# Short-sequence attention on one core: four rows of a head per partition, float32 loads rounded on GpSimd, eight heads per exp

## The chip, the cores and the metric

The kernel runs on one core of a Trainium2 chip. A core has five engines with queues of their own: TensorE (PE, with its weight loads listed apart as PEld), VectorE (DVE), ScalarE (ACT), GpSimd (POOL) and SyncE (SP, which here only issues DMAs). Data lie in SBUF and PSUM, both of 128 partitions; PSUM has 8 banks of 2 KB per partition, and matmuls write only there. The metric is the time of one execution in microseconds (us), the median of several.

## The reference

32 batches of 12 heads, sequence length 128, head size 64, all float32:

```python
scale = 1.0 / np.sqrt(q.shape[-1])
scores = scale * np.matmul(q, k.transpose(0, 1, 3, 2))
scores_max = np.max(scores, axis=-1, keepdims=True)
attn = np.exp(scores - scores_max)
attn = attn / (np.sum(attn, axis=-1, keepdims=True) + 1e-8)
return np.matmul(attn, v).astype(np.float32)
```

The inputs are small (a normal draw times 0.1), so both kernels leave out the maximum.

## The kernel before

It loops over the 32 batches. In each, three DMAs from GpSimd's queue bring q, k and v of all 12 heads to SBUF and round them to bfloat16 on the way (`q_bf`, `k_bf`, `v_bf`, 128 partitions, one sequence row of every head per partition, so a DMA moves pieces of 64 float32 values, 256 B). `v_bf` has a 65th column of ones per head; its matmul gives the sum of the exponentials for free.

Two heads at a time are transposed on PE (`qt_ps`, `kt_ps`, one buffer each in PSUM) and copied to SBUF, q by ACT (L68) and k by DVE (L75). For groups of 4 heads the scores are formed, keys on partitions, with a contraction of 64 (L84, `sT_ps`, four PSUM banks, one buffer); one exp on ACT takes the four heads (L92, `attnT`). The output matmuls (L103) go two heads at a time into `o_ps` (two banks, one buffer), and DVE copies them out to `o_b` (L110). At the end of a batch come a reciprocal of the sums (L116), a multiply (L118) and one store from SP's queue (L119).

The order on each engine is not that of the text. The framework's scheduler lays all instructions out in advance, by the order of the text as priority and by what its model of the engines says is ready, and puts in all semaphores; PE therefore mixes transposes of the next batch with scores and outputs of this one. At run time each engine follows that fixed order.

Of the kernel before, what the change touches and what calls it, by code (L numbers as in the profile page):

```python
# [1 line left out]

# [5 lines left out]


@with_exitstack
def kernel(
    ctx: ExitStack,
    tc: tile.TileContext,
    q: bass.AP,
    k: bass.AP,
    v: bass.AP,
    out: bass.AP,
):
    nc = tc.nc  # L20
    f32 = mybir.dt.float32
    bf16 = mybir.dt.bfloat16

    B, H, S, D = q.shape
    assert S == 128 and D == 64
    scale = 1.0 / (D ** 0.5)
    HT = 128 // D
    NP = H // HT
    HX = 4
    HO = 2  # L30
    BANK = 512

    qr = q.rearrange("b h s d -> b s h d")
    kr = k.rearrange("b h s d -> b s h d")
    vr = v.rearrange("b h s d -> b s h d")
    orr = out.rearrange("b h s d -> b s h d")

    singles = ctx.enter_context(tc.tile_pool(name="singles", bufs=1))
    ident = singles.tile([128, 128], bf16)
    make_identity(nc, ident)  # L40

    pbf = ctx.enter_context(tc.tile_pool(name="pbf", bufs=3))
    pt = ctx.enter_context(tc.tile_pool(name="pt", bufs=3))
    pa = ctx.enter_context(tc.tile_pool(name="pa", bufs=6))
    po = ctx.enter_context(tc.tile_pool(name="po", bufs=2))
    ps_t = ctx.enter_context(tc.tile_pool(name="ps_t", bufs=1, space=bass.MemoryType.PSUM))
    ps_s = ctx.enter_context(tc.tile_pool(name="ps_s", bufs=1, space=bass.MemoryType.PSUM))
    ps_o = ctx.enter_context(tc.tile_pool(name="ps_o", bufs=1, space=bass.MemoryType.PSUM))

    for b in range(B):  # L50
        q_bf = pbf.tile([128, H, D], bf16, tag="q_bf")
        nc.gpsimd.dma_start(out=q_bf, in_=qr[b])  # L52
        k_bf = pbf.tile([128, H, D], bf16, tag="k_bf")
        nc.gpsimd.dma_start(out=k_bf, in_=kr[b])  # L54
        v_bf = pbf.tile([128, H, D + 1], bf16, tag="v_bf")
        nc.gpsimd.memset(v_bf[:, :, D:D + 1], 1.0)  # L56
        nc.gpsimd.dma_start(out=v_bf[:, :, :D], in_=vr[b])  # L57

        qt = pt.tile([128, NP, 128], bf16, tag="qt")
        kt = pt.tile([128, NP, 128], bf16, tag="kt")  # L60
        for p in range(NP):
            qt_ps = ps_t.tile([128, 128], bf16, tag="qt_ps")
            nc.tensor.transpose(  # L63
                qt_ps,
                q_bf[:, p * HT:(p + 1) * HT, :].rearrange("a b c -> a (b c)"),
                ident,
            )
            nc.scalar.copy(qt[:, p, :], qt_ps)  # L68
            kt_ps = ps_t.tile([128, 128], bf16, tag="kt_ps")
            nc.tensor.transpose(  # L70
                kt_ps,
                k_bf[:, p * HT:(p + 1) * HT, :].rearrange("a b c -> a (b c)"),
                ident,
            )
            nc.vector.tensor_copy(kt[:, p, :], kt_ps)  # L75

        o_b = po.tile([128, H, D + 1], f32, tag="o_b")

        for g in range(H // HX):
            sT_ps = ps_s.tile([128, HX, BANK], f32, tag="sT")  # L80
            for i in range(HX):
                h = g * HX + i
                p, j = divmod(h, HT)
                nc.tensor.matmul(  # L84
                    sT_ps[:, i, :128],
                    lhsT=kt[j * D:(j + 1) * D, p, :],
                    rhs=qt[j * D:(j + 1) * D, p, :],
                    start=True,
                    stop=True,
                )  # L90
            attnT = pa.tile([128, HX, 128], bf16, tag="attnT")
            nc.scalar.activation(  # L92
                out=attnT,
                in_=sT_ps[:, :, :128],
                func=mybir.ActivationFunctionType.Exp,
                bias=0.0,
                scale=scale,
            )
            for gg in range(HX // HO):
                o_ps = ps_o.tile([128, HO, BANK], f32, tag="o_ps")  # L100
                for i in range(HO):
                    h = g * HX + gg * HO + i
                    nc.tensor.matmul(  # L103
                        o_ps[:, i, :D + 1],
                        lhsT=attnT[:, gg * HO + i, :],
                        rhs=v_bf[:, h, :],
                        start=True,
                        stop=True,
                    )
                nc.vector.tensor_copy(  # L110
                    o_b[:, g * HX + gg * HO:g * HX + (gg + 1) * HO, :],
                    o_ps[:, :, :D + 1],
                )

        recip = po.tile([128, H], f32, tag="recip")
        nc.vector.reciprocal(recip, o_b[:, :, D:D + 1])  # L116
        o_sb = po.tile([128, H, D], f32, tag="o_sb")
        nc.vector.tensor_mul(o_sb, o_b[:, :, :D], recip.to_broadcast([128, H, D]))  # L118
        nc.sync.dma_start(out=orr[b], in_=o_sb)  # L119


# [1 line left out]
_INS = ['q', 'k', 'v']  # L123
_OUTS = [((32, 12, 128, 64), 'float32')]


# [23 lines left out]
```

## Time and profile before

| | |
|---|---|
| median of 3 runs | 226.65 us (226.57 to 226.68) |
| span of the profiled execution, first to last instruction | 224.4 us |
| its own time beside the span | not listed apart; the median is 2.25 us above the span |
| PE busy | 168.3 us (75%), 1152 matmuls |
| DVE, ACT, POOL busy | 120.2, 99.7, 101.5 us |
| granted TensorE clock | 1.000 |
| HBM read, written | 37.75, 12.58 MB |

A row of a group reads: line, engine, operation, output and inputs by the program's names, shapes, count, then busy time in us and the mean of one in ns, then the idle time of the engine just before these instructions and what ended it. A row of the timeline reads: start in us, length in us, engine, line, operation, names, shapes, how many were merged into the row. A row of the waits reads: who waited for whom, us in total, times, longest. For PE `64*128` is the part of the array in use, rows by columns. A matmul's length holds the time that its data take to pass the array, so lengths of matmuls overlap, and their starts tell more. A row by windows reads: stretch, its length, busy time and count for each engine, granted clock, DMA share, GB/s.

### The profile page before, as it was taken

What the parts mean: (1) busy time and instruction counts of PE and PEld (TensorE: products, weight loads), DVE (VectorE), ACT (ScalarE), POOL (GpSimd) and SP (SyncE); (2) the same over time, 40 slices, a digit from 0 to 9 for tenths busy, and PEclk for the clock granted to TensorE, in tenths of its full rate; (3) what the DMA queues carried; (4) which work ended last, traced back from release to release, by engine and by line L of the source; (5) the groups of instructions that cost most, each with busy time, mean ns of one, the idle gap of its engine ahead of it and who ended that gap; (6) DMA issues with size and microseconds to landing.
All of it is one profiled execution on the core that took longest, in us unless ns stands there. A gap on an engine that the chain in (4) does not pass through costs nothing.

```text
span 224.4 us, 3513 instructions
## 1 busy us (share of the span) xinstructions
PE 168.3 (75%) x1152; PEld 83.1 (37%) x1152; DVE 120.2 (54%) x448; ACT 99.7 (44%) x289; POOL 101.5 (45%) x134
## 2 busy tenths in 40 slices
PE   0688787788787787877787877788877778878750
PEld 0344333344333343333343333444333334333330
DVE  0264555664555564555564555565555565456652
ACT  2554545445544445444445444444444444444320
POOL 8963455534475443455443455543355534222000
DMA  7999999999999999999999999999999999999333
GB/s 50 149 156 184 148 142 140 155 148 166 151 153 161 161 159 166 148 149 141 129 151 167 146 148 134 137 154 167 149 146 144 135 150 161 142 110 134 76 69 71
DMA packets 198674, 31.69 MB, mean 141 GB/s; under 512 B 198656, under 2 KB 198656, under 8 KB 198656
## 3 DMA queue, kind: packets, MB, share of 16 engines
q0 software_dynamic: 148992, 18.88, 131.9%
q1 hardware_dynamic: 49664, 12.58, 31.0%
q8 instruction: 9, 0.15, 0.3%
q14 instruction: 9, 0.07, 0.1%
HBM read 37.75 MB, written 12.58 MB: 224 GB/s over the span
## 4 chain that ended last, share of the span: by engine, by line
PE 64%; ACT 17%; DVE 9%; issue 6%; DMA 2%; ACTq 0%; POOL 0%; POOLq 0%
PE sT_ps L84 26%; PE qt_ps L63 14%; PE o_ps L103 14%; PE kt_ps L70 11%; ACT attnT L92 9%; ACT qt L68 7%; DVE o_b L110 5%; DVE kt L75 3%; DMA q_bf<-in_q_dram 2%; DVE o_sb L118 1%; ACTq L92 0%; DVE recip L116 0%; POOL ident masks.py:197 0%; POOLq masks.py:199 0%; POOLq L134 0%
## 5 line engine op out<-in xcount | busy, mean ns | idle before, releaser
L68 ACT COPY qt<-qt_ps 128x128 bf16<-128x128 bf16 x192 | 50.4, 263 | 69.0 <-PE qt_ps L63 69.0
L75 DVE COPY kt<-kt_ps 128x128 bf16<-128x128 bf16 x192 | 42.8, 223 | 70.8 <-PE kt_ps L70 66.1
L84 PE MATMUL sT_ps<-qt,kt 64*128 64x128 bf16 x384 | 71.5, 282 | 12.2 <-ACT attnT L92 11.5
L92 ACT ACTIVATE attnT<-sT_ps 128x512 bf16<-128x512 f32 x96 | 57.3, 597 | 47.7 <-PE sT_ps L84 42.9
L63 PE MATMUL qt_ps<-ident,q_bf 128*128 128x128 bf16 x192 | 54.2, 282 | 26.8 <-ACT qt L68 21.4
L110 DVE COPY o_b<-o_ps 128x130 f32<-128x130 f32 x192 | 55.6, 289 | 29.2 <-PE o_ps L103 28.9
L103 PE MATMUL o_ps<-v_bf,attnT 128*128 128x65 bf16 x384 | 56.8, 242 | 6.1 <-DVE o_b L110 6.1
L70 PE MATMUL kt_ps<-ident,k_bf 128*128 128x128 bf16 x192 | 56.4, 294 | 5.3 <-DVE kt L75 4.5
L84 PEld LDWEIGHTS <-kt 64*128 64x128 bf16 x384 | 26.4, 101 | 61.1 <-issue 43.0
L103 PEld LDWEIGHTS <-attnT 128*128 128x128 bf16 x384 | 34.3, 120 | 34.4 <-issue 26.5
L56 POOL MEMSET v_bf<- 128x12 bf16 x32 | 5.0, 155 | 79.9 <-PE o_ps L103 79.9
L52 POOL DMA_DIRECT2D q_bf<-in_q_dram x32 | 32.6, 1020 | 10.2 <-PE qt_ps L63 8.9
L57 POOL DMA_DIRECT2D v_bf<-in_v_dram x32 | 32.6, 1018 | 9.9 <-POOL v_bf L56 9.9
L54 POOL DMA_DIRECT2D k_bf<-in_k_dram x32 | 32.8, 1025 | 1.4 <-PE kt_ps L70 1.4
L63 PEld LDWEIGHTS <-q_bf 128*128 128x128 bf16 x192 | 18.9, 113 | 31.4 <-issue 15.7
L118 DVE TENSOR_TENSOR o_sb<-o_b,recip 128x768 f32<-128x768 f32 x32 | 30.3, 948 | 0.0
L70 PEld LDWEIGHTS <-k_bf 128*128 128x128 bf16 x192 | 23.2, 121 | 8.7 <-issue 0.9
L116 DVE RECIPROCAL recip<-o_b 128x12 f32<-128x12 f32 x32 | 7.0, 219 | 0.0
L68 ACT ACT_TABLE_LOAD x1 | 1.3, 1283 | 0.7 <-PEq L134 0.7
masks.py:199 POOL TENSOR_SCALAR_AFFINE_SELECT ident<-ident 128x128 bf16<-128x128 bf16 x1 | 0.3, 305 | 0.1
masks.py:197 POOL MEMSET ident<- 128x128 bf16 x1 | 0.2, 204 | 0.3 <-POOLq L134 0.3
L134 POOL MEMSET const-float32-0.0<- 128x1 f32 x1 | 0.1, 98 | 0.2 <-issue 0.2
(3 smaller groups left out, 0.3 us busy)
## 6 DMA issues: line engine op xcount, KB each, us to landing
out_dram<-o_sb SPq DMA_DIRECT2D x32, 384.0 KB, 5.7
q_bf<-in_q_dram POOLq DMA_DIRECT2D x32, 192.0 KB, 5.9
k_bf<-in_k_dram POOLq DMA_DIRECT2D x32, 192.0 KB, 6.4
v_bf<-in_v_dram POOLq DMA_DIRECT2D x32, 192.0 KB, 5.1
```

The costliest lines, as they stand in the source:

```text
L52: nc.gpsimd.dma_start(out=q_bf, in_=qr[b])
L54: nc.gpsimd.dma_start(out=k_bf, in_=kr[b])
L57: nc.gpsimd.dma_start(out=v_bf[:, :, :D], in_=vr[b])
L63: nc.tensor.transpose(qt_ps, q_bf[:, p * HT:(p + 1) * HT, :].rearrange("a b c -> a (b c)"), ident,)
L68: nc.scalar.copy(qt[:, p, :], qt_ps)
L70: nc.tensor.transpose(kt_ps, k_bf[:, p * HT:(p + 1) * HT, :].rearrange("a b c -> a (b c)"), ident,)
L75: nc.vector.tensor_copy(kt[:, p, :], kt_ps)
L84: nc.tensor.matmul(sT_ps[:, i, :128], lhsT=kt[j * D:(j + 1) * D, p, :], rhs=qt[j * D:(j + 1) * D, p, :], start=True, stop=True,)
L92: nc.scalar.activation(out=attnT, in_=sT_ps[:, :, :128], func=mybir.ActivationFunctionType.Exp, bias=0.0, scale=scale,)
L103: nc.tensor.matmul(o_ps[:, i, :D + 1], lhsT=attnT[:, gg * HO + i, :], rhs=v_bf[:, h, :], start=True, stop=True,)
L110: nc.vector.tensor_copy(o_b[:, g * HX + gg * HO:g * HX + (gg + 1) * HO, :], o_ps[:, :, :D + 1],)
L118: nc.vector.tensor_mul(o_sb, o_b[:, :, :D], recip.to_broadcast([128, H, D]))
```

## The change

All four tensors are viewed as slabs: 4 neighbouring rows of a head in each partition (1 KB in one piece), 4 heads in 128 partitions. A load brings 4 slabs (16 heads) of q, k or v as float32, 512 KB, from SP's queue, two loads ahead. GpSimd rounds them to bfloat16, q and k in two instructions each, so that two slabs lie side by side, v in one. The unit of work is then 8 heads (2 slabs), 48 units in all.

In `front(u)` eight transposes fill one PSUM bank (`qk_ps`) and DVE copies it out in one instruction (`qkT`). The transposed columns of a head come in the order (row within the partition, partition). Keys need the same order in v, so 16 matmuls with 32 columns of the identity as weights select and place the rows of v in `v_ps`; ACT copies them to `v_e`, whose columns of ones were written once. Eight score matmuls fill two banks (`s_ps`, two buffers), and one exp on ACT takes all 8 heads. In `back(u - 1)` the output matmuls of the unit before run, 32 of them, each with 32 columns of `attnT` as weights and 65 columns of `v_e`, so that the result lies as the slabs do. Reciprocal and multiply read PSUM directly, and a store of 16 heads follows every second unit.

The core of the diff, with the copies and views of the old kernel cut:

```diff
-    for b in range(B):
-        q_bf = pbf.tile([128, H, D], bf16, tag="q_bf")
-        nc.gpsimd.dma_start(out=q_bf, in_=qr[b])
...
+    def load(l):
+        sl = slice(l * LU * US, (l + 1) * LU * US)
+        got = []
+        for nm, src in (("q_f", qs), ("k_f", ks), ("v_f", vs)):
+            t = pf.tile([128, LU * US, R * D], f32, tag=nm)
+            nc.sync.dma_start(out=t, in_=src[:, sl, :])
+            got.append(t)
+        loaded[l] = got
...
+        for nm, src in (("q_b", q_f), ("k_b", k_f)):
+            t = pb.tile([128, LU * UP, R, 2, D], bf16, tag=nm)
+            for ab in range(2):
+                nc.gpsimd.tensor_copy(
+                    t[:, :, :, ab, :],
+                    src.rearrange("p (i ab) (r d) -> p i ab r d", ab=2, r=R)[:, :, ab, :, :],
+                )
+            got.append(t)
+        t = pb.tile([128, LU * US, R * D], bf16, tag="v_b")
+        nc.gpsimd.tensor_copy(t, v_f)
...
+        qk_ps = ps_t.tile([128, 2, UP, R, R, SP], bf16, tag="qk_ps")
+        for j, src in enumerate((q_b, k_b)):
+            for i in range(UP):
+                for r in range(R):
+                    nc.tensor.transpose(
+                        qk_ps[:, j, i, :, r, :],
+                        src[:, w * UP + i, r, :, :].rearrange("p a d -> p (a d)"),
+                        ident,
+                    )
+        qkT = pt.tile([128, 2, UP, R, 128], bf16, tag="qkT")
+        nc.vector.tensor_copy(qkT, qk_ps.rearrange("p j i h r s -> p j i h (r s)"))
+
+        v_ps = ps_v.tile([128, R, US, D], f32, tag="v_ps")
+        for h in range(R):
+            for r in range(R):
                 nc.tensor.matmul(
+                    v_ps[r * SP:(r + 1) * SP, h, :, :],
+                    lhsT=ident[:, h * SP:(h + 1) * SP],
+                    rhs=v_b[:, w * US:(w + 1) * US, r * D:(r + 1) * D],
                     start=True,
                     stop=True,
                 )
+        v_e = v_es[u % NVE]
+        nc.scalar.copy(v_e[:, :, :, :D], v_ps)
+
+        s_ps = ps_s.tile([128, 2, UP, R, 128], f32, tag="s_ps")
+        for i in range(UP):
+            for h in range(R):
+                for ab in range(2):
+                    pr = slice(ab * D, (ab + 1) * D)
                     nc.tensor.matmul(
+                        s_ps[:, ab, i, h, :],
+                        lhsT=qkT[pr, 1, i, h, :],
+                        rhs=qkT[pr, 0, i, h, :],
                         start=True,
                         stop=True,
                     )
+        attnT = pa.tile([128, 2, UP, R, 128], bf16, tag="attnT")
+        nc.scalar.activation(out=attnT, in_=s_ps, func=EXP, bias=0.0, scale=scale)
+        stage[u] = (v_e, attnT)
...
+        o_ps = ps_o.tile([128, 2, 512], f32, tag="o_ps")
+        for b2 in range(2):
+            for c in range(4):
+                n, r = divmod(b2 * 4 + c, R)
+                i, ab = divmod(n, 2)
+                for h in range(R):
+                    nc.tensor.matmul(
+                        o_ps[h * SP:(h + 1) * SP, b2, c * (D + 1):(c + 1) * (D + 1)],
+                        lhsT=attnT[:, ab, i, h, r * SP:(r + 1) * SP],
+                        rhs=v_e[:, h, n, :],
+                        start=True,
+                        stop=True,
+                    )
+        o4 = o_ps[:, :, :4 * (D + 1)].rearrange("p b (c e) -> p b c e", e=D + 1)
+        recip = po.tile([128, 2, 4], f32, tag="recip")
+        nc.vector.reciprocal(recip, o4[:, :, :, D])
+        nc.vector.tensor_mul(
+            o_sb[:, w].rearrange("p (b c) d -> p b c d", b=2),
+            o4[:, :, :, :D],
+            recip.unsqueeze(3).to_broadcast([128, 2, 4, D]),
+        )
...
+    load(0)
+    load(1)
+    for u in range(NU + 1):
+        if u < NU:
+            l, w = divmod(u, LU)
+            if w == 0:
+                if l + 2 < NL:
+                    load(l + 2)
+                to_bf16(l)
+            front(u)
+        if u >= 1:
+            back(u - 1)
```

Here `R = 4`, `SP = 32`, `UH = 8` heads per unit, `US = 2` slabs, `UP = 1` pair of slabs, `LU = 2` units per load, `NL = 24` loads, `NU = 48` units. The pool of float32 tiles has 4 buffers per name, that of bfloat16 tiles 3; `qk_ps` and `v_ps` take one PSUM bank each, `s_ps` two buffers of two banks, `o_ps` two banks.

More of the change, by code (lines that the diff above doesn't have):

```diff
@@ L22 @@
     bf16 = mybir.dt.bfloat16
+    EXP = mybir.ActivationFunctionType.Exp
     B, H, S, D = q.shape
@@ L26, with slabs @@
     scale = 1.0 / (D ** 0.5)
[L27 to L36, printed above, removed]
+    R = 4
+    SP = S // R
+    UH = 8
+    US = UH // R
+    UP = US // 2
+    LU = 2
+    NL = B * H // (UH * LU)
+    NU = NL * LU
+    def slabs(t):
+        x = t.rearrange("b h s d -> (b h s) d")
+        return x.rearrange("(n p r) d -> p n (r d)", p=128, r=R)
+    qs, ks, vs, os_ = slabs(q), slabs(k), slabs(v), slabs(out)
     singles = ctx.enter_context(tc.tile_pool(name="singles", bufs=1))
@@ L40 @@
     make_identity(nc, ident)
-    pbf = ctx.enter_context(tc.tile_pool(name="pbf", bufs=3))
+    NVE = 4
+    v_es = []
+    for i in range(NVE):
+        t = singles.tile([128, R, US, D + 1], bf16, name=f"v_e{i}")
+        nc.gpsimd.memset(t[:, :, :, D:D + 1], 1.0)
+        v_es.append(t)
+    pf = ctx.enter_context(tc.tile_pool(name="pf", bufs=4))
+    pb = ctx.enter_context(tc.tile_pool(name="pb", bufs=3))
     pt = ctx.enter_context(tc.tile_pool(name="pt", bufs=3))
-    pa = ctx.enter_context(tc.tile_pool(name="pa", bufs=6))
@@ L48 @@
     ps_o = ctx.enter_context(tc.tile_pool(name="ps_o", bufs=1, space=bass.MemoryType.PSUM))
-    for b in range(B):
-        q_bf = pbf.tile([128, H, D], bf16, tag="q_bf")
[L52 to L83, printed above, removed]
@@ new lines, with to_bf16 @@
+    loaded = {}
+    cast = {}
+    def load(l):
[6 more added lines that the diff above has]
+        loaded[l] = got
+    def to_bf16(l):
+        q_f, k_f, v_f = loaded.pop(l)
+        got = []
+        for nm, src in (("q_b", q_f), ("k_b", k_f)):
[8 more added lines that the diff above has]
+        nc.gpsimd.tensor_copy(t, v_f)
+        got.append(t)
+        cast[l] = got
@@ L84 @@
                 nc.tensor.matmul(
-                    sT_ps[:, i, :128],
-                    lhsT=kt[j * D:(j + 1) * D, p, :],
-                    rhs=qt[j * D:(j + 1) * D, p, :],
+                    v_ps[r * SP:(r + 1) * SP, h, :, :],
+                    lhsT=ident[:, h * SP:(h + 1) * SP],
+                    rhs=v_b[:, w * US:(w + 1) * US, r * D:(r + 1) * D],
                     start=True,
@@ L90 @@
                 )
[L91 to L102, printed above, removed]
+        v_e = v_es[u % NVE]
[5 more added lines that the diff above has]
+                    pr = slice(ab * D, (ab + 1) * D)
                     nc.tensor.matmul(
-                        o_ps[:, i, :D + 1],
-                        lhsT=attnT[:, gg * HO + i, :],
-                        rhs=v_bf[:, h, :],
+                        s_ps[:, ab, i, h, :],
+                        lhsT=qkT[pr, 1, i, h, :],
+                        rhs=qkT[pr, 0, i, h, :],
                         start=True,
@@ L109 @@
                     )
[L110 to L119, printed above, removed]
+        attnT = pa.tile([128, 2, UP, R, 128], bf16, tag="attnT")
@@ new lines, in front, with back @@
+        nc.scalar.activation(out=attnT, in_=s_ps, func=EXP, bias=0.0, scale=scale)
+        stage[u] = (v_e, attnT)
+    osb = {}
+    def back(u):
+        l, w = divmod(u, LU)
+        v_e, attnT = stage.pop(u)
+        if w == 0:
+            osb[l] = po.tile([128, LU, UH, D], f32, tag="o_sb", name="o_sb")
+        o_sb = osb[l]
+        o_ps = ps_o.tile([128, 2, 512], f32, tag="o_ps")
[19 more added lines that the diff above has]
+        )
+        if w == LU - 1:
+            nc.sync.dma_start(
+                out=os_[:, l * LU * US:(l + 1) * LU * US, :],
+                in_=o_sb.rearrange("p w (n r) d -> p (w n) (r d)", r=R),
+            )
+            del osb[l]
@@ L123 @@
+    load(0)
+    load(1)
+    for u in range(NU + 1):
+        if u < NU:
+            l, w = divmod(u, LU)
+            if w == 0:
+                if l + 2 < NL:
[4 more added lines that the diff above has]
+            back(u - 1)
 _INS = ['q', 'k', 'v']
```

9 lines of the change are left out of this document (7 added, 2 removed).

## The prediction

> **What bounds the kernel now.** I read the page first: shares by engine, the chain that ended last, the groups. Then the waits, the timeline of PE, and the DMA in one stretch.
>
> ```profile
> PE 64%; ACT 17%; DVE 9%; issue 6%; DMA 2%; ACTq 0%; POOL 0%; POOLq 0%
> ...
> 109.31 0.61 ACT attnT L92
> 115.98 0.61 ACT attnT L92
> ...
> PEld L84 <- issue: 43.0, 100, 0.7
> PEld L103 <- issue: 26.5, 65, 0.8
> PE qt_ps L63 <- ACT qt L68: 21.4, 61, 0.4
> PEld L63 <- issue: 15.7, 31, 0.5
> PE sT_ps L84 <- ACT attnT L92: 11.5, 36, 0.6
> PE qt_ps L63 <- DMA q_bf<-in_q_dram: 5.3, 1, 5.3
> ```
>
> The same exp of two neighbouring batches lies 6.67 us apart: 12 heads per 6.67 us, 32 times 213 us of the span. PE holds 64% of the chain. It waits for a DMA once, at the start, so transfers are hidden today. It waits 21.4 and 11.5 us because a PSUM buffer is still being read, and its weight loads stand 85 us (43.0, 26.5, 15.7) before nothing that the profile names. The timeline says what that is:
>
> ```profile
> 99.88 0.28 PE L84 MATMUL sT_ps<-qt,kt 64*128 64x128 bf16 x1
> 100.10 0.29 PE L63 MATMUL qt_ps<-ident,q_bf 128*128 128x128 bf16 x1
> 100.18 0.31 PE L70 MATMUL kt_ps<-ident,k_bf 128*128 128x128 bf16 x1
> 100.43 0.29 PE L84 MATMUL sT_ps<-qt,kt 64*128 64x128 bf16 x2
> 100.65 0.29 PE L103 MATMUL o_ps<-v_bf,attnT 128*128 128x65 bf16 x2
> 100.75 0.30 PE L63 MATMUL qt_ps<-ident,q_bf 128*128 128x128 bf16 x1
> 100.84 0.31 PE L70 MATMUL kt_ps<-ident,k_bf 128*128 128x128 bf16 x1
> ```
>
> Starts are what counts here. Within one array shape (128*128) a transpose is followed after 0.08 to 0.09 us (100.10, 100.18; 100.75, 100.84), and two 65-column matmuls and the next one after them start within 0.10 us (100.65 to 100.75): 0.05 us each. Two score matmuls (64*128, the two halves of the array rows) take 0.29 us together where one takes 0.28: they start together. But each change between 64*128 and 128*128 takes 0.22 to 0.25 us from start to start: of that 0.15 us is more than the work (0.25 less 0.08; 0.22 less 0.08). PE is thus bound by emptying at each change of shape and by one-deep PSUM, not by matmuls.
>
> **The change part by part.** 384 heads become 48 units of 8 heads.
>
> PE, per unit. (1) 8 transposes: 8 x 0.08 = 0.65 us. (2) 16 new selection matmuls of 128 columns, each on 32 array columns; nothing before uses part of the columns. Nearest row below: the score pair, which starts together; then four column groups run side by side, 4 x 0.08 = 0.33 us. Above: none overlap, 16 x 0.08 = 1.3 us. I take 0.5, near the pair, as it is the only case of parts of the array at work together. (3) 8 score matmuls, 4 pairs: 0.33 us. (4) The output matmuls go from 1 to 4 per head, 32 per unit, again on 32 columns: 8 x 0.05 = 0.4 us side by side, 32 x 0.05 = 1.6 us one by one; I take 0.9, since at 65 columns the issue of 64 instructions weighs more than the columns. (5) Shape changes: transposes, selections, scores, outputs, 4 per unit at 0.15 = 0.6 us; before there were several per microsecond. (6) The scores wait for the copy of qk_ps: it takes 0.7 us (below) and 0.3 us of matmul latency, and the selections cover 0.5 and a shape change; output matmuls of the unit before can fill the rest where the order puts them there. I take 0.2 us, between 0 and 0.6. Sum 0.65 + 0.5 + 0.33 + 0.9 + 0.6 + 0.2 = 3.18 us; with everything side by side 2.3, with nothing 4.7 (no wait is left then, as the selections cover it, 4.5). The waits for PSUM go: qk_ps, v_ps and o_ps are still one deep, but each is read once in 3.2 us, and the readers need about 1 us.
>
> ```profile
> L68 ACT COPY qt<-qt_ps 128x128 bf16<-128x128 bf16 x192 | 50.4, 263 | 69.0 <-PE qt_ps L63 69.0
> L75 DVE COPY kt<-kt_ps 128x128 bf16<-128x128 bf16 x192 | 42.8, 223 | 70.8 <-PE kt_ps L70 66.1
> L92 ACT ACTIVATE attnT<-sT_ps 128x512 bf16<-128x512 f32 x96 | 57.3, 597 | 47.7 <-PE sT_ps L84 42.9
> L110 DVE COPY o_b<-o_ps 128x130 f32<-128x130 f32 x192 | 55.6, 289 | 29.2 <-PE o_ps L103 28.9
> L118 DVE TENSOR_TENSOR o_sb<-o_b,recip 128x768 f32<-128x768 f32 x32 | 30.3, 948 | 0.0
> L116 DVE RECIPROCAL recip<-o_b 128x12 f32<-128x12 f32 x32 | 7.0, 219 | 0.0
> L52 POOL DMA_DIRECT2D q_bf<-in_q_dram x32 | 32.6, 1020 | 10.2 <-PE qt_ps L63 8.9
> masks.py:199 POOL TENSOR_SCALAR_AFFINE_SELECT ident<-ident 128x128 bf16<-128x128 bf16 x1 | 0.3, 305 | 0.1
> masks.py:197 POOL MEMSET ident<- 128x128 bf16 x1 | 0.2, 204 | 0.3 <-POOLq L134 0.3
> L134 POOL MEMSET const-float32-0.0<- 128x1 f32 x1 | 0.1, 98 | 0.2 <-issue 0.2
> ```
>
> DVE: 289 ns at 130 and 948 at 768 float32 elements give 1.03 ns an element on 155 ns; the bf16 copy of 128 from PSUM (223 ns) fits half of that slope. The qkT copy of 1024 is then 0.68 us (1.2 at full slope), the multiply of 512 0.68, the reciprocal 0.22: 1.6 to 2.1 us a unit, under 3.18. ACT: 263 at 128 and 597 at 512 give 0.87 ns an element, so 0.60 for the v copy and 1.04 for the exp of 1024: 1.64 us. Both lie beside PE. On DVE the copy of unit u stands behind the multiply of an earlier unit, 0.9 us that run beside the transposes; on ACT the v copy stands behind an exp whose results are needed two stages later.
>
> POOL loses its 96 DMA issues (1.02 us each) and memsets. It gains, per 2 units, 4 casts of 512 elements and one of 1024. No cast is in the trace; 204 less 98 ns over 127 elements of a memset is 0.83 ns, 305 less 98 over 128 of the select 1.6 ns. So 3072 x 0.83 to 1.6 + 5 x 0.1 = 3.0 to 5.4 us; I take 4.2, between, as a cast reads like the select and computes less. PE needs 6.4 us for 2 units, so the casts are hidden; uncovered at the start only. Above 1.9 ns an element POOL would be the bound.
>
> [...]
>
> ```profile
> HBM read 37.75 MB, written 12.58 MB: 224 GB/s over the span
> ...
> q0 software_dynamic: 148992, 18.88, 131.9%
> ...
> 8.00:17.00 9.00, 7.78 (x60) 4.15 (x59) 4.91 (x20) 5.09 (x15) 7.06 (x10) 1.00 2.44 155
> ...
> L119 SPq DMA_DIRECT2D out_dram<-o_sb x32: 372/372/412, 17.1 to 220.3; - x32
> ```
>
> DMA: q0's bytes are counted after rounding, 18.88 MB for 37.75 MB read. From 8 to 17 us only loads run (the first store is issued at 17.1): 155 GB/s rounded is 310 GB/s read, in pieces of 256 B. The change reads and writes the same 50.33 MB in pieces of 1 KB, a quarter as many. At the rate of 310 it is 162 us of transfers, as much as PE: a slower rate is not likely with fewer pieces, a faster one may be, but no row shows 1 KB. This is a second bound beside the first. The cast in the DMA goes. SP issues 72 loads and 24 stores, 96 x 0.37 = 36 us, alone on its queue; a store there waits for its multiply, and the loads behind it with it. They are issued two loads ahead (4 units, 13 us), against 5 to 6 us to landing, so this costs nothing; were the lead gone, casts would wait and PE behind them.
>
> ```profile
> 5.30 0.29 PE L63 MATMUL qt_ps<-ident,q_bf 128*128 128x128 bf16 x1 [5.30 <-DMA q_bf<-in_q_dram]
> ...
> 219.34 0.96 DVE L118 TENSOR_TENSOR o_sb<-o_b,recip 128x768 f32<-128x768 f32 x1
> ```
>
> Start: q landed at 5.3 us. Now each of q, k, v is 512 KB, 1.7 us at 310 GB/s, on one queue; q at about 5, k 6.7, v 8.4; two casts of 0.75 us follow q and two k, so transposes end at about 8.6. End: after the last scores the exp (1.04), then reciprocal and multiply (0.9); from the end of the last multiply (220.3) to the end of the span (224.4) 4.1 us: 6 in all.
>
> **Sum.** 8.6 + 48 x 3.18 + 6 = 167 us of span by PE; DMA gives 162 us with some 3 before the first bytes, the same. Two bounds that tie hold each other up a little; I add 3. The profiled span before is 224.4 and the median 226.65, so 2.25 lie around it: 172 us.
>
> [...]
>
> **Rivals.** (B) Column groups fully side by side and 1 KB pieces faster: PE 2.3 to 2.7 us a unit, DMA above 350 GB/s; 48 x 2.6 + 14.6 + 2.25 = 142, or 144 + 9 + 2.25 = 155 by DMA: 142 to 158. For it: the pairs. Against: both must hold, and stores mix with loads. (C) Outputs and selections overlap little: PE 3.6 to 4.4 us, 190 to 228; for it, each still loads its own weights, 128 instructions a unit. [...] (D) Slower: no overlap at all in the 48 column-group matmuls, at one by one 0.08 and 0.05 us, 4.7 us a unit: 226 + 14.6 + 2.25 = 243. It decides from 4.37 us a unit on, (226.65 - 16.9) / 48. For it: three times as many matmuls; against: the pairs. POOL would do the same from 2.7 ns an element. (E) The change frees PE but transfers stay the bound at 310 GB/s: 169, inside my forecast.
>
> **Chances.** Forecast (158 to 190, with E) 0.55, B 0.15, C 0.19 (the cast rule in it), D 0.09, no change 0.02. Time 172; the range 150 to 210 leaves out about 0.06 below and 0.14 above. Faster by over 0.2% (what a measurement here can tell) 0.89, within it 0.02, slower 0.09.
>
> **What would show it.** In the changed profile: starts of output matmuls under 0.03 us apart (right) or 0.05 (C, D); about 4 shape changes a unit, and weight loads standing under 40 us; transposes, scores and selections at the same place in each 3.2 us; casts under 6.4 us per 2 units, else PE waits for POOL; GB/s about 300. Wrong it would be made by casts over 1.9 ns an element, by column groups in single file, by an order that changes shape more than 6 times a unit, or by transfers well over 310 GB/s beside a PE unit of 2.5 us.

## The result, and the profile after

| | before | after |
|---|---|---|
| median of 5 runs each, us | 226.65 (226.55 to 226.80) | 175.17 (172.06 to 177.99) |
| profiled execution, us (span) | (224.4) | 177.99 (176.2) |
| ratio after / before, 95% interval | | 0.762 (0.759 to 0.765) |

The ratio compares undisturbed runs alone (172 and 173 us for the changed kernel), so it lies below the quotient of the medians. The forecast was 172 in a range of 150 to 210, "faster" at 0.89: time and sign came out as said. The sum behind them did not: several of its terms were wrong, in opposite directions, so that the time was met in part by luck.

The page of the changed kernel, busy time, granted clock by fortieths of the span, queues, and the chain that ended last:

```profile
PE 124.9 (71%) x3072; PEld 86.2 (49%) x3072; DVE 74.2 (42%) x144; ACT 76.4 (43%) x97; POOL 82.3 (47%) x130
...
PEclk9999996879555855555555556999555579975555
...
q8 instruction: 24, 0.39, 0.8%
...
HBM read 37.75 MB, written 12.58 MB: 286 GB/s over the span
...
PE 48%; DVE 29%; DMA 10%; issue 8%; ACT 1%; POOL 1%; SPq 1%; ACTq 0%
```

PE's share of the chain fell from 64% to 48%, DVE's rose from 9% to 29%. Two rows had no counterpart in the prediction. The clock row (`PEclk`, tenths of full speed) stands at or near half in most slices from the seventh on; what its first slices mean is told below. And a queue named "instruction" brings 24 packets, 0.39 MB, so 16 KB each (before: 9).

The groups on the other engines (busy us, mean ns | idle before):

```profile
L82 POOL CAST t<-t 128x512 bf16<-128x512 f32 x96 | 56.4, 616 | 59.4 <-DMA t<-in_q_dram 38.7
L121 ACT CAST v_e<-v_ps 128x512 bf16<-128x512 f32 x48 | 28.3, 589 | 73.4 <-PE v_ps L113 73.2
L136 ACT ACTIVATE attnT<-s_ps 128x1024 bf16<-128x1024 f32 x48 | 49.3, 1026 | 19.9 <-PE s_ps L128 19.5
L108 DVE COPY qkT<-qk_ps 128x1024 bf16<-128x1024 bf16 x48 | 33.1, 690 | 50.6 <-PE qk_ps L102 50.4
...
L163 DVE TENSOR_TENSOR o_sb<-o_ps,recip 128x512 f32<-128x512 f32 x48 | 33.2, 692 | 1.7
...
L88 POOL CAST t<-t 128x1024 bf16<-128x1024 f32 x24 | 25.0, 1042 | 14.2 <-DMA t<-in_v_dram 11.2
```

ACT 0.59 and 1.03 us (said 0.60, 1.04), DVE 0.69 twice (said 0.68). A cast costs (1042 - 616) / 512 = 0.83 ns an element, the lower end of the bounds 0.83 to 1.6: 4 x 0.616 + 1.042 = 3.5 us per two units, where 4.2 was taken.

PE over two units at full clock, in order of starts:

```profile
19.74 0.21 PE L153 MATMUL o_ps<-v_e,attnT 128*32 128x65 bf16 x2 [0.76 <-issue]
19.88 0.62 PE L102 MATMUL qk_ps<-ident,t 128*128 128x128 bf16 x8
20.43 0.41 PE L113 MATMUL v_ps<-t,ident 128*32 128x128 bf16 x16
21.06 0.39 PE L153 MATMUL o_ps<-v_e,attnT 128*32 128x65 bf16 x27 [0.23 <-DVE o_sb L163]
21.57 0.40 PE L128 MATMUL s_ps<-qkT 64*128 64x128 bf16 x8
...
22.07 0.62 PE L102 MATMUL qk_ps<-ident,t 128*128 128x128 bf16 x8
...
26.04 0.21 PE L153 MATMUL o_ps<-v_e,attnT 128*32 128x65 bf16 x3 [1.74 <-issue]
```

Sixteen selections take 0.41 us and 27 outputs 0.39 us: column groups do run side by side. Among the outputs the median start is 4 ns after the one before. Transposes of successive units lie 2.19 us apart (19.88, 22.07), far under the 3.18 predicted. Then PE stands 1.74 us, and 0.76 us before this unit, for nothing that the trace names. Counted through the trace, those gaps fall at matmul 222, 349, 476, 603, 730, 857 and 985: every 127 or 128 matmuls, that is every 256 instructions of PE with the weight loads, as they fall in two units. Each ends about 2.3 us after a 16 KB packet on the instruction queue begins (packets at 17.40, 23.70, 29.86 us; gaps end at 19.74, 26.04, 32.06). The next packet begins 3.8 to 4.0 us after such a gap has ended (19.74 to 23.70, 26.04 to 29.86). At full clock the kernel thus moves by one such packet per two units, every 6.0 to 6.3 us.

Later, at half clock, the chain of work that ended last (start us, length us, what) is another:

```profile
84.21 0.98 PE qk_ps L102 x8
...
85.21 0.70 DVE qkT L108
...
85.96 0.61 PE s_ps L128 x6
86.57 0.59 PE o_ps L153 x24
87.18 0.22 DVE recip L162
87.42 0.70 DVE o_sb L163
...
88.26 0.40 PE o_ps L153 x11
88.67 0.55 PE qk_ps L102 x4
...
89.24 0.70 DVE qkT L108
...
89.99 0.60 PE s_ps L128 x5
90.59 0.55 PE v_ps L113 x16
91.14 0.22 PE s_ps L128
91.36 0.98 PE qk_ps L102 x8
```

Two units take 7.15 us (84.21 to 91.36): 4.50 us of PE, 2.32 us of DVE, the rest hand-overs. No DMA is in it, and no gap of the first kind: PE and DVE take turns at `qk_ps` and `o_ps`, which are one deep. The length of one score matmul tells the clock (ns, least, median, most). The first row is of the kernel before, the second of the changed one, the third of the run without later loads told below:

```profile
L84 PE MATMUL sT_ps<-qt,kt x384: 260/285/311, 8.1 to 216.2; 64*128 64x128 bf16 x192
```

```profile
L128 PE MATMUL s_ps<-qkT x384: 216/287/312, 10.6 to 168.9; 64*128 64x128 bf16 x192
```

```profile
L131 PE MATMUL s_ps<-qkT x384: 213/216/311, 10.6 to 117.2; 64*128 64x128 bf16 x192
```

The shape is the same in all three. In the changed kernel it takes 216 to 227 ns where the records say full clock (one of 112 is 285), 262 to 312 where they say half. The kernel before never had one under 260. Its page holds no clock row, and the "1.000" listed for it means that no record exists. The start of the changed kernel shows that this isn't full clock: its first record stands at 16.73 us, the stretch ahead of it is listed as 1.00 too, and yet its score matmuls are long:

```profile
L128 PE MATMUL s_ps<-qkT x24: 283/310/311, 10.6 to 16.3; 64*128 64x128 bf16 x24
```

So by these lengths (260 to 311 ns, beside 262 to 312 where half clock is recorded) the kernel before ran at half clock throughout. That is inferred from lengths, not recorded. The run without the later loads, whose records say full clock from 16.4 to 118.8 us, has a median of 216 ns, the kernel before one of 285.

**Putting the time together**, roughly. With the prediction's 14.6 us of start and end and the 1.8 us between span and time (177.99 - 176.2), all at the full-clock pace gives 24 x 6.2 + 16.4 = 165, all at the half-clock pace 24 x 7.15 + 16.4 = 188. The mean clock of 0.693 counts the first 16.7 us, which have no record, as full. Behind them it is 0.66:

```profile
16.73:176.20 159.47, 117.24 (x2917) 80.77 (x2912) 71.25 (x139) 71.22 (x91) 72.48 (x107) 0.66 0.87 285
```

The records hold 1.0 and 0.5 alone, so that is full clock for 0.32 x 159.5 = 51 us, 29% of the span, and 1 / (0.29 / 148.8 + 0.71 / 171.6) + 16.4 = 181 us; measured 177.99. The run of 172.06 us had clock 0.761; with as long a start at half the same working gives 178. The two paces give the size of the time, 2 to 3% too high, and no more.

### The profile page after: what moved, and what is told of

Read it like the earlier page. It is cut to its first block, busy times and chain, and to the rows that moved or that the text cites. A ratio compares the mean times of both kernels' runs of the same rounds, so it can differ in the third digit from the quotient of the medians.

```text
span 176.2 us, 6901 instructions
## 1 busy us (share of the span) xinstructions
PE 124.9 (71%) x3072; PEld 86.2 (49%) x3072; DVE 74.2 (42%) x144; ACT 76.4 (43%) x97; POOL 82.3 (47%) x130
## 4 chain that ended last, share of the span: by engine, by line
PE 48%; DVE 29%; DMA 10%; issue 8%; ACT 1%; POOL 1%; SPq 1%; ACTq 0%
PE s_ps L128 15%; PE qk_ps L102 14%; DVE qkT L108 14%; PE o_ps L153 12%; DVE o_sb L163 11%; DMA out_dram<-o_sb 6%; PE v_ps L113 6%; DMA t<-in_v_dram 4%; DVE recip L162 3%; POOL t L88 1%; ACT attnT L136 1%; SPq L72 1%; ACT v_e L121 0%; ACTq L136 0%
## 5 line engine op out<-in xcount | busy, mean ns | idle before, releaser
L82 POOL CAST t<-t 128x512 bf16<-128x512 f32 x96 | 56.4, 616 | 59.4 <-DMA t<-in_q_dram 38.7
L121 ACT CAST v_e<-v_ps 128x512 bf16<-128x512 f32 x48 | 28.3, 589 | 73.4 <-PE v_ps L113 73.2
L136 ACT ACTIVATE attnT<-s_ps 128x1024 bf16<-128x1024 f32 x48 | 49.3, 1026 | 19.9 <-PE s_ps L128 19.5
L108 DVE COPY qkT<-qk_ps 128x1024 bf16<-128x1024 bf16 x48 | 33.1, 690 | 50.6 <-PE qk_ps L102 50.4
L153 PE MATMUL o_ps<-v_e,attnT 128*32 128x65 bf16 x1536 | 34.7, 227 | 22.3 <-DVE o_sb L163 13.3
L102 PE MATMUL qk_ps<-ident,t 128*128 128x128 bf16 x384 | 45.8, 279 | 6.2 <-POOL t L82 6.2
L128 PE MATMUL s_ps<-qkT 64*128 64x128 bf16 x384 | 30.6, 278 | 15.3 <-DVE qkT L108 11.4
L102 PEld LDWEIGHTS <-t 128*128 128x128 bf16 x384 | 30.8, 124 | 12.0 <-POOL t L82 6.4
L163 DVE TENSOR_TENSOR o_sb<-o_ps,recip 128x512 f32<-128x512 f32 x48 | 33.2, 692 | 1.7
L88 POOL CAST t<-t 128x1024 bf16<-128x1024 f32 x24 | 25.0, 1042 | 14.2 <-DMA t<-in_v_dram 11.2
L113 PE MATMUL v_ps<-t,ident 128*32 128x128 bf16 x768 | 26.6, 280 | 3.0 <-POOL t L88 2.7
```

What stands on the lines that cost most here:

```text
L82: nc.gpsimd.tensor_copy(t[:, :, :, ab, :], src.rearrange("p (i ab) (r d) -> p i ab r d", ab=2, r=R)[:, :, ab, :, :],)
L88: nc.gpsimd.tensor_copy(t, v_f)
L102: nc.tensor.transpose(qk_ps[:, j, i, :, r, :], src[:, w * UP + i, r, :, :].rearrange("p a d -> p (a d)"), ident,)
L108: nc.vector.tensor_copy(qkT, qk_ps.rearrange("p j i h r s -> p j i h (r s)"))
L113: nc.tensor.matmul(v_ps[r * SP:(r + 1) * SP, h, :, :], lhsT=ident[:, h * SP:(h + 1) * SP], rhs=v_b[:, w * US:(w + 1) * US, r * D:(r + 1) * D],
L121: nc.scalar.copy(v_e[:, :, :, :D], v_ps)
```

## The experiments

Theory at the start, "loop": half or more of a unit is hand-over between PE, DVE and ACT through one-deep PSUM, transfers hidden. Rival: loads and stores, 50.33 MB, bind by themselves. The third theory, PE's own instruction stream, came from these first runs.

**1. The later loads left out.** The casts go on, from the first two loads; q, k and v of later units are those of the first two loads.

```diff
+        if l >= 2:
+            loaded[l] = loaded[l - 2]
+            return
...
-        q_f, k_f, v_f = loaded.pop(l)
+        q_f, k_f, v_f = loaded[l]
```

> Loads 2 to 23 are left out: the units work on the data of the first two loads, casts and stores stay. Theory (loop: PE and DVE hand one-deep PSUM tiles to each other, transfers are not the bound): the spacing of about 7.15 us per 2 units at half clock stays, only the stalls of PE that the profile names issue (12 us in all) and part of the start go: 158 to 172 us. Rival (transfers bind at 290 to 340 GB/s): below 150 us.

125.09 us, ratio 0.550 (0.547 to 0.554). A row by windows (stretch, length, busy us of PE, PEld, DVE, ACT, POOL, clock, DMA share, GB/s), and one of its waits:

```profile
30.00:60.00 30.00, 25.18 (x885) 17.94 (x884) 20.85 (x42) 22.10 (x28) 23.27 (x36) 1.00 0.36 127
```

```profile
PE o_ps L156 <- issue: 1.9, 5, 0.4
```

The time is in the rival's range. Counted through the trace, the engines alone do two units in 4.38 us at best, so the loop theory as put (158 to 172) fell. The records have full clock from 16.4 to 118.8 us, and unnamed gaps are 1.9 us though the same 24 packets come: the loads lie behind both. They need not be the bound themselves for that.

**2. Transfers alone.** Same loads and stores, no matmuls and no casts; a DVE copy in place of the arithmetic.

```diff
+        nc.vector.tensor_copy(o_sb[:, :, 0:8], q_f[:, :, 0:8])
+        nc.vector.tensor_copy(o_sb[:, :, 8:16], k_f[:, :, 0:8])
+        nc.vector.tensor_copy(o_sb[:, :, 16:R * D], v_f[:, :, 16:R * D])
+        nc.sync.dma_start(out=os_[:, l * LU * US:(l + 1) * LU * US, :], in_=o_sb)
```

> All 72 loads and 24 stores stay, the computation is left out: each store takes a copy of parts of the loaded tiles. Theory (loop): transfers by themselves need 130 to 148 us, 350 to 390 GB/s, as in the fastest slices of the changed kernel's profile. Rival (transfers bind): 160 to 172 us, 300 to 320 GB/s, the rate that the prediction took from 256 B pieces.

138.25 us, ratio 0.609 (0.608 to 0.611).

```profile
HBM read 37.75 MB, written 12.58 MB: 371 GB/s over the span
```

385 GB/s in the steady part, not the 310 of the prediction. Neither engines alone (125) nor transfers alone (138) give 175, so something holds the kernel back only when both run. The lower clock is a part of it: 0.979 without the later loads, 0.693 with them.

**3 and 4. Where the PSUM banks go.** `o_ps` two deep and `s_ps` one; then `qk_ps` and `v_ps` two deep and `s_ps` one.

```diff
-    ps_s = ctx.enter_context(tc.tile_pool(name="ps_s", bufs=2, ...
+    ps_s = ctx.enter_context(tc.tile_pool(name="ps_s", bufs=1, ...
-    ps_o = ctx.enter_context(tc.tile_pool(name="ps_o", bufs=1, ...
+    ps_o = ctx.enter_context(tc.tile_pool(name="ps_o", bufs=2, ...
```

> o_ps gets two buffers, s_ps one instead of two. Theory (loop): output matmuls no longer wait for the multiply (13.3 us of waits and the multiply's 11% of the chain), scores may now wait for the exp: 160 to 170 us. Rival (transfers): no change, 172 to 178 us.

172.17 us (167.85 to 173.65), overlapping the 172.06 to 177.99 of the change: no difference can be claimed. The 13.3 us of waits for the multiply went, but scores now waited 18.9 us for `qkT` (11.4 in the change). At full clock the gaps stayed, every 128 matmuls and 6.20 us apart (they end at 20.04, 26.24, 32.43, 38.63 us).

```diff
-    ps_t = ctx.enter_context(tc.tile_pool(name="ps_t", bufs=1, ...
-    ps_s = ctx.enter_context(tc.tile_pool(name="ps_s", bufs=2, ...
-    ps_v = ctx.enter_context(tc.tile_pool(name="ps_v", bufs=1, ...
+    ps_t = ctx.enter_context(tc.tile_pool(name="ps_t", bufs=2, ...
+    ps_s = ctx.enter_context(tc.tile_pool(name="ps_s", bufs=1, ...
+    ps_v = ctx.enter_context(tc.tile_pool(name="ps_v", bufs=2, ...
```

> qk_ps and v_ps get two buffers each, s_ps one instead of two. Theory (loop): transposes of the next unit can run beside the copy of this one, so scores find their qkT ready (11.4 us of waits of PE and 14% of the chain in that copy): 158 to 170 us. Rival (transfers): no change, 172 to 178 us.

179.61 us, ratio 0.794 (0.789 to 0.799): slower than the change, and both expectations missed. PE now waited 14.2 us for the exp to free `s_ps`, and unnamed gaps were 15.8 us (11.7 in the change). Depth of PSUM is thus not what caps the full-clock pace. At half clock two units took about 7.0 us in the first of these runs and 6.9 in the second, beside 7.15; but each took a buffer from `s_ps`, so what depth alone would bring isn't shown.

**5. More PE instructions, hardly more work.** 16 selections of 2 columns a unit ahead of the real ones, 160 PE instructions a unit for 128.

```diff
+                nc.tensor.matmul(
+                    v_ps[r * SP:(r + 1) * SP, h, 0, 0:2],
+                    lhsT=ident[:, h * SP:(h + 1) * SP],
+                    rhs=v_b[:, w * US, r * D:r * D + 2],
```

> Ahead of each unit's 16 selection matmuls stand 16 more with the same weights and 2 columns each, whose results are overwritten: 128 PE instructions per unit become 160, with hardly more array work. Theory (fetch: PE runs dry after each 256 of its instructions until the next 16 KB of its program have come, and while loads run that takes 6.0 to 6.2 us from block to block): 32 blocks instead of 24, 32 x 6.2 and 17 for start and end, 205 to 225 us. Rival (array and PSUM hand-over set the pace, at a low clock): 16 x 5 to 30 ns a unit, 178 to 196 us.

186.36 us (182.56 to 186.72).

```profile
q8 instruction: 30, 0.49, 1.0%
...
PE 47%; issue 22%; DVE 16%; DMA 6%; ACT 5%; POOL 1%; SPq 0%; ACTq 0%
```

The time lies in the rival's range, the pattern is the theory's: 30 packets for 24, gaps at matmul 223, 350 and so on as before, 37.2 us of unnamed gaps on PE instead of 11.7, and "issue" with 22% of the chain instead of 8%. The expectation counted too many microseconds a packet.

**6. v loaded in key order**, four DMAs with pieces of 256 B, no selections and no ACT copy (POOL rounds straight into `v_e`).

```diff
+        for r in range(R):
+            nc.sync.dma_start(out=t[r * SP:(r + 1) * SP, :, :], in_=vk[r, :, hs, :])
```

> Undoes v's part: v is loaded in key order in pieces of 256 B (four DMAs a load), GpSimd rounds it straight to v_e; the 16 selection matmuls and ScalarE's copy go. 96 PE instructions per unit, 18 blocks. Theory (fetch): 18 x 6.2 + 17 = 129, so transfers take over: 142 to 160 us. Rival (PSUM hand-over at half clock, 7.15 us per 2 units less the selections' 0.55 and a shape change each): 5.7 x 24 + 14, 150 to 165 us with nothing changed in the stalls at each 256 instructions; transfers of 256 B binding: 165 us and over.

185.27 us (181.95 to 188.34). The ranges of the theory and of the hand-over rival were missed; the time lies in the last case, 256 B transfers binding (165 and over). It is longer than the change's, so the change's part for v, taken whole, pays. No clock row here either; score matmuls last 282 to 311 ns, so half clock throughout. No unnamed gaps. The chain:

```profile
PE 33%; DVE 28%; DMA 24%; SPq 6%; issue 4%; POOL 3%; POOLq 0%
```

In the steady stretches PE and DVE take turns, 7.05 us per two units; transfers (270 GB/s over the span) are now in the chain with 24%.

**7. Outputs in full width**: 8 matmuls of 128 weight columns a unit instead of 32 of 32, and four stores in pieces of 256 B.

```diff
-                for h in range(R):
-                        o_ps[h * SP:(h + 1) * SP, b2, c * (D + 1):(c + 1) * (D + 1)],
-                        lhsT=attnT[:, ab, i, h, r * SP:(r + 1) * SP],
+                    o_ps[:, b2, c * (D + 1):(c + 1) * (D + 1)],
+                    lhsT=attnT[:, ab, i, h, :],
```

> Undoes the output's part: 8 output matmuls of 128 weight columns per unit instead of 32 of 32; a partition then holds one row of 8 heads, and stores go out in pieces of 256 B by four DMAs. 80 PE instructions per unit, 15 blocks. Theory (fetch): 15 x 6.2 + 17 = 110, so transfers set the time: 142 to 158 us. Rival (PSUM hand-over at half clock): the output matmuls take as long or longer, 8 x 0.05 us, 168 to 180 us.

184.78 us, ratio 0.813 (0.809 to 0.817): both expectations missed. 15 packets, no unnamed gaps, and still slower:

```profile
PEclk9999995867555555555567855555555587555555
...
DMA 26%; PE 22%; DVE 18%; SPq 11%; ACT 10%; POOL 6%; issue 4%; POOLq 0%; ACTq 0%
```

Half clock nearly throughout, and DMA and SP's queue in the chain, where four stores stand ahead of the next loads. Fewer instructions did not help while clock and transfers got worse; this run and the one before it change two things each and can't price one alone.

**8. No casts** but for the first two loads. Later units use those; loads go on, each read by a cast of 8 columns.

```diff
+        if l >= 2:
+            for x in (q_f, k_f, v_f):
+                tiny = pt.tile([128, 8], bf16, tag="tiny")
+                nc.gpsimd.tensor_copy(tiny, x[:, 0, 0:8])
+            cast[l] = cast[l - 2]
+            return
```

> Loads and stores stay, but only the first two loads are rounded; of each later tile GpSimd reads 8 elements, and all units work on the data of the first two loads. Theory (fetch; casts of 3.5 us per 2 units are hidden): 168 to 178 us. Rival (casts late behind their loads hold PE up, as the prediction's cast case would): below 160 us.

157.92 us (154.56 to 161.88); in the profiled execution clock 0.84, 329 GB/s, unnamed gaps 14.6 us. Below 160, as the rival had it, some 17 us under the change (175.17 - 157.92). That isn't the price of the casts alone: the units here wait for no later load either, and the clock is higher. Nor is it the rival's path: in the change matmuls wait for a cast only three times, all in the first 10.1 us (6.2 and 2.7 us).

**9. Two matmuls more a unit**, 512 columns each, into `v_ps` ahead of the selections, which overwrite them: does PE work as such hold the clock up?

```diff
+        for _ in range(2):
+            nc.tensor.matmul(
+                v_ps.rearrange("p h n d -> p (h n d)"),
+                lhsT=ident,
+                rhs=v_b[:, w * US:(w + 1) * US, :].rearrange("p n x -> p (n x)"),
```

> Behind the transposes of each unit stand two matmuls of 128 x 128 by 512 columns into v_ps, which the selections then overwrite: 4 PE instructions more per unit and 0.43 us of array work at full clock, 0.86 us at half. Theory (clock: at a granted clock of 0.5 PE and DVE need 7.15 us for 2 units, at 1.0 with loads running about 6.0, so more PE activity pays by lifting the clock): clock above 0.9 in the profile and 158 to 170 us. Rival (PE's own work sets the time whatever the clock): 185 to 215 us.

170.61 us, ratio 0.751 (0.748 to 0.754) beside 0.762 (0.759 to 0.765) for the change.

```profile
PEclk9999999978999999699599959999999999759996
...
PE 45%; DVE 24%; issue 17%; DMA 8%; ACT 2%; POOL 1%; SPq 1%; ACTq 0%
```

By the steps of the change's transposes (0.107 us per 128 columns at half clock, 0.056 at full) the two matmuls are, as an estimate, 0.86 and 0.45 us of PE a unit. More matmul work and no more time, at the edge of what the clock theory had (158 to 170): the clock's mean rises from 0.693 to 0.931 (behind the start without records from 0.66 to 0.92). But what half clock had hidden comes out: "issue" doubles to 17% of the chain, 23.3 us of gaps, at every 125 to 127 matmuls. Two bounds, one behind the other.

**10. The change's loads alone, in the kernel before**: float32 from SP's queue, casts on POOL, three buffers.

```diff
-        nc.gpsimd.dma_start(out=q_bf, in_=qr[b])
+        q_f = pf.tile([128, H, D], f32, tag="q_f")
+        nc.sync.dma_start(out=q_f, in_=qr[b])
+        nc.gpsimd.tensor_copy(q_bf, q_f)
```

> The kernel before with one part of the change alone: q, k, v come as float32 from SP's queue (still 256 B pieces) and GpSimd rounds them, three casts of 768 elements a batch. Theory (transfers are hidden in the kernel before, PE's shape changes and one-deep PSUM set its time): 220 to 232 us. Rival (loads off GpSimd's queue give a part of the gain): below 215 us.

353.77 us, ratio 1.561 (1.559 to 1.563): both expectations missed, by 120 us. Its waits, and a stretch of its chain:

```profile
SPq L126 <- DVE o_sb L125: 190.8, 30, 9.9
...
POOL v_bf L64 <- DMA v_f<-in_v_dram: 77.7, 19, 6.4
```

```profile
139.41 0.15 POOL v_bf L61
...
141.59 6.32 DMA v_f<-in_v_dram
...
147.96 0.84 POOL v_bf L64
...
148.85 0.28 PE o_ps L110 x2
```

The load of v stands on SP's queue behind the store of an earlier batch (issued at 141.12), which waits for that batch's multiply; its cast and the outputs wait for the load. POOL's casts in turn stand behind the memset of `v_bf`, which waits for outputs. The change gives its loads a lead of two in the text, and this kernel doesn't; that the lead is what is missing here is argued, as no run adds it.

**11. The change's wide transposes alone, in the kernel before**: six transposes into one bank, one copy for q and one for k a batch instead of six each.

```diff
+        qt_ps = ps_t.tile([128, NP, 128], bf16, tag="qt_ps")
+        kt_ps = ps_t.tile([128, NP, 128], bf16, tag="kt_ps")
+        for src, dst in ((q_bf, qt_ps), (k_bf, kt_ps)):
+            for p in range(NP):
...
+        nc.scalar.copy(qt, qt_ps)
+        nc.vector.tensor_copy(kt, kt_ps)
```

> The kernel before with another part alone: the 6 transposes of q and the 6 of k each fill one PSUM bank and are copied out by one instruction (ScalarE for q, VectorE for k). Theory (the gain comes from fewer shape changes and hand-overs on PE): 165 to 200 us. Rival (PE's order stays mixed by its other one-deep buffers, or loads take over): 212 to 228 us.

212.22 us, ratio 0.935 (0.929 to 0.940). The chain and a wait:

```profile
DMA 31%; POOL 20%; PE 19%; issue 17%; ACT 6%; DVE 5%; POOLq 0%; ACTq 0%
...
PE qt_ps L65 <- DMA q_bf<-in_q_dram: 12.4, 8, 5.5
```

The time lies at the lower edge of the rival's range (212 to 228). With PE relieved, the old loads take over at once: DMA goes from 2% to 31% of the chain. They were hidden in the kernel before, but closely behind PE, so this part of the change alone brought 6.5% of the time.

**12. Fewer PE instructions at the same work**: number 9 with the selections of two units made together, 16 of 256 columns instead of 32 of 128. 232 PE instructions per two units for 264.

```diff
-                    rhs=v_b[:, w * US:(w + 1) * US, r * D:(r + 1) * D],
+                    rhs=v_b[:, :, r * D:(r + 1) * D],
```

> On the kernel with the two fillers per unit: the selections of two units are made together, 16 matmuls of 256 columns per 2 units instead of 32 of 128, half of them behind the scores of the first unit; array work and transfers stay as they were, PE's instructions per 2 units fall from 264 to 232. Theory (fetch: at full clock PE waits for its program, 6.0 to 6.6 us for each 256 instructions while loads run): 12% fewer blocks, 148 to 160 us. Rival (hand-over between PE, DVE and ScalarE sets the pace): 165 to 174 us.

158.83 us (157.19 to 161.53), ratio 0.697 (0.695 to 0.700): faster than both kernels.

```profile
q8 instruction: 21, 0.34, 0.9%
```

```profile
30.00:60.00 30.00, 22.61 (x627) 15.32 (x637) 16.56 (x34) 17.56 (x23) 16.22 (x25) 1.00 1.08 358
```

This is inside the 148 to 160 of the theory of the instruction stream, not the rival's 165 to 174. Unnamed gaps fell from 23.3 to 6.5 us, and the rate in the steady part rose to 358 GB/s, near the 385 of transfers alone. The profiled clock rose as well (0.931 to 0.969), so the instruction count needn't be the whole of the gain.

The packets against PE's instructions (matmuls and weight loads, as many of the one as of the other), and PE's unnamed gaps ("issue" in the waits of its matmuls, summed):

| kernel | PE instructions | / 256 | packets | gaps, us |
|---|---|---|---|---|
| before | 2304 | 9.0 | 9 | 0 |
| outputs in full width | 3840 | 15.0 | 15 | 0 |
| v in key order | 4608 | 18.0 | 18 | 0 |
| wide selections | 5568 | 21.8 | 21 | 6.5 |
| after | 6144 | 24.0 | 24 | 11.7 |
| after, later loads left out | 6144 | 24.0 | 24 | 1.9 |
| after with two matmuls more | 6336 | 24.8 | 24 | 23.3 |
| after with tiny selections | 7680 | 30.0 | 30 | 37.2 |

The trace doesn't say what a packet holds. In all eight kernels their number is that of PE's instructions by 256, rounded down (9 for 2304, 24 for 6144, 30 for 7680). That they bring PE's own program while the kernel runs is the author's inference from this match and the queue's name; no run shows it directly. More instructions gave more gaps, fewer gave fewer, a higher clock at nearly the same count gave more, and without loads beside them the gaps nearly went. There a packet began 1.8 us (median) after PE had come to the next block of 256; in the changed kernel, at the first six gaps, 3.8 to 4.9 us. The gaps are thus best read as late packets, which is inferred too.

## Why the prediction was right, and where it was not

Point by point, in its own order:

- **Transposes.** 8 x 0.08 read the step behind the first transpose after a change of shape. In a row of eight it is 0.08 us once and then 0.107 at half clock, and 0.066 and then 0.056 at full: 0.98 and 0.55 us in place of 0.65.
- **Side by side.** Held: selections took 0.41 us at full clock and 0.62 at half (0.5 taken, 0.33 to 1.3), 32 outputs about 0.45 and 0.63 us (0.9 taken, 0.4 to 1.6). The outputs' term was mis-sized by a factor of 1.4 to 2: the argument that 64 instructions' issue outweighs the columns was wrong at this place.
- **Shape changes.** 237 changes in the trace, 4.9 a unit (4 said), 506 before. From start to start they take 0.18 to 0.24 us at half clock, as before, and 0.13 to 0.16 at full. Held. That the array empties at a change, as the prediction put it, isn't shown: the trace has the times between starts.
- **"The waits for PSUM go."** Failed. At half clock 2.32 us of DVE per two units, 1.16 a unit, stand in the chain, where the term for such waits was 0.2. "Each is read once in 3.2 us, and the readers need about 1 us" overlooked that PE and the reader take turns where nothing else is left for PE to do, so the reader's time adds to PE's. That depth alone would mend this isn't shown (numbers 3 and 4).
- **3.18 us a unit.** Right in size by compensation. It is 2.19 with nothing else in the way, 3.0 to 3.15 at full clock with the instruction packets, 3.58 at half clock. The sum held no term for gaps at the packets of the instruction queue (3072 matmuls for 1152, 24 packets for 9) and none for the clock, which stood in its table as 1.000. The durations it took from the kernel before were, by the lengths of its score matmuls, half-clock ones. The time was met because a term that was priced too high (the outputs) and those put too low or at nothing nearly cancelled; that is luck.
- **DMA at 310 GB/s, 162 us.** Failed: 138 us alone, 385 GB/s. The rate of 256 B pieces was carried over to 1 KB pieces although "a faster one may be" stood in the text. "Two bounds that tie" was therefore not the state of things.
- **Casts hidden.** The price came out at the lower bound, 0.83 ns an element. PE waits for casts at the start only, as said; but without the casts and the wait for later loads the kernel takes 158 us, and which of the two gives that isn't settled.
- **SP's order costs nothing.** Not shown. SP stands 98.3 us behind stores that wait for their multiply, and number 10 shows what such an order can cost. No run here took the store off SP's queue.
- **Rivals.** B's two conditions came true, column groups side by side and transfers above 350 GB/s (385 alone; 286 over the changed kernel's span), and B's time did not, as the two unlisted bounds took the gain. C and D fell: a unit's 48 column-group matmuls overlap (16 selections 0.41 us, 27 outputs 0.39). The chances count a cast rule within C, which no run shows; a cast took 0.83 ns an element. E's time (169) was near, but transfers that take 138 us alone weren't the bound.

What the profile of before could have told: 9 packets on the instruction queue for 2304 PE instructions, which the change's count turns into 24. Its matmul lengths tell of the clock only beside the records of the change.

**Open.** What decides the clock: in the changed kernel it is 0.50 from 66 to 102 us with PE busy 29.85 of 36 us, while the run without later loads has PE busy 25.18 of 30 us at 1.00, so busy share alone doesn't tell them apart; two matmuls more a unit raised it. Why a packet begins later beside the loads. And whether the casts or the wait for later loads cost the 17 us of number 8, and by which path.

## What to carry to other kernels

Count PE instructions as well as PE time: here matmuls on 32 columns were each nearly free (16 selections in 0.41 us), but at full clock PE paused at every 256 of its instructions, 6.0 to 6.3 us from one pause to the next, and one selection over 256 columns in place of two over 128 brought 170.61 us to 158.83 (clock 0.931 and 0.969). Judge the clock by the length of a known matmul (here 216 ns at full, 262 to 312 at half), not by a missing record, and price a step that PE must wait for as writer plus reader. When a kernel moves from one bound to another, parts of a change tried alone can lose (1.56) or win little (0.935) where the whole wins 0.762.

## What the runs showed of the hardware that was not expected

- The queue named "instruction" brought one packet of 16 KB for each 256 PE instructions in eight kernels (24 for 6144 in the change); beside loads at some 350 GB/s PE moved on by one packet every 6.0 to 6.3 us at full clock.
- The granted clock stayed at half with PE busy 83% of a stretch (29.85 us of 66 to 102), and two 512-column matmuls more a unit raised its mean from 0.693 to 0.931 (0.66 to 0.92 where records exist) without costing time.
- A multiply of 768 elements on DVE took 1182 ns beside GpSimd's casts, 948 without them, where the multiply was the same; a cast of k took 1140 ns in the mean, 820 ns where it ran alone and 1560 ns beside a multiply. What makes the two slower together, no run shows.

```profile
L125 DVE TENSOR_TENSOR o_sb<-o_b,recip 128x768 f32<-128x768 f32 x32 | 37.8, 1182 | 1.1
...
L59 POOL CAST k_bf<-k_f 128x768 bf16<-128x768 f32 x32 | 36.5, 1140 | 3.9 <-DMA k_f<-in_k_dram 3.7
```
